# Layer norms that scale and split two feature blocks per operation, and an output projection whose last part accumulates onto a seeded PSUM bank

## The chip, the cores and the metric

The kernel runs on one core of one Trainium2 chip. A core has a matrix engine (TensorE, PE in the profile; its weight loads are the row PEld), three engines for elementwise work (VectorE is DVE, ScalarE is ACT, GpSimd is POOL) and SyncE (SP), which only issues DMAs here. Each engine works through its own queue in order and waits on semaphores for the others. Matmuls write to PSUM; everything else lies in SBUF. The metric is the device time of one execution in microseconds, lower is better.

## The reference

One inference step of a hybrid encoder layer over 576 tokens (512 of a prompt, 64 of a sample), model width 1024:

```
h   = x @ W_in                                  # heads of two kinds of attention
mix = concat(ForgettingAttention, SparseAttention)     # 1024 wide
x   = LN1(alpha * x + mix @ W_o)
x   = LN2(alpha * x + relu(x @ W_up)^2 @ W_down)       # hidden width 4096
x   = x + sigmoid(x @ W_g + b_g) * (p @ W_ple)
LN(x) = (x - mean(x)) * rsqrt(var(x) + eps) * g + b    # over the 1024 features of a token
```

All data are float32. The two layer norms, the `mix @ W_o` in front of LN1 and what surrounds them are what matters here.

## The kernel before

**Layout.** Features lie on the partitions, tokens along the free dimension: `Y` is 128 x 8 x 576, eight blocks `j` of 128 features. A token half is 288 wide (`A` is tokens 0 to 287, `B` the rest; for LN2 `A2` is 256 and `B2` 320 wide). Every matmul operand is split into a high part (rounded to the reduced format of the matmul) and a low part (the rest), and a product is three matmuls: high x high, high x low, low x high. `BH` and `BL` are the two parts of the activations; `whl` holds both parts of a weight block, made from the DMA's `wraw` by one ScalarE cast (L149) and one VectorE subtraction (L155).

**The stretch around LN1.** `wo1` multiplies six of the eight 128-row blocks of `W_o` and adds ALPHA times the residual, so that `Y` holds the residual with most of the projection. `wo2(hs, ln, steps)` does the last two row blocks for one token half: for each pair of feature blocks twelve matmuls into one PSUM tile, then VectorE adds that tile to `Y` (L1263), and the layer norm's running sum over the blocks is updated (`ln.add`). `wo2` runs for half A, then for half B, then `ple()` computes `p @ W_ple`: eight feature blocks, twelve matmuls each, and ScalarE copies each result to `PL` (L1276). Then `up(0)` starts the feed-forward: half A, then half B, and in each half the features are taken in four pairs `kp`, all four output blocks per pair.

**The layer norm** (`LayerNorm.steps`) runs beside these matmuls, one step per yield. TensorE forms the mean with a matmul by a constant (L1180), VectorE subtracts it (L1184), ScalarE squares (L1186, L1189), VectorE sums (L1190, L1159), TensorE forms the variance (L1200), ScalarE and VectorE its inverse root (L1202, L1203), TensorE spreads it over the partitions (L56, `n<-ident,ln_r`), into PSUM. Then for each pair of feature blocks: `scale` multiplies by `g` and by the inverse root, `high` adds `b` and rounds into `BH`, `low` adds `b` and subtracts `BH` into `BL`. All three take one feature block per instruction because `g` and `b` are one column each. Last, `bias` adds `b` to `Y` itself.

**PSUM tiles in turn.** `psum_g()` hands out three tiles in turn: two of one pool (`m`) and, on every third call from the second on, one of another (`psB`). Calls 1 to 4 are `wo2(A)`, 5 to 8 `wo2(B)`, 9 to 16 the eight blocks of `ple`, 17 and 18 the two tiles of `up(0)` on half A. A tile can be written again only when the instruction that empties it is done: call 11 waits for what empties call 8, and call 17 (a `psB` tile) for what empties call 14, which is block 5 of `ple`.

**What sets the order.** The code is written as generators that are interleaved (`drive`), evacuations are queued with `later`, and a scheduler then puts each engine's instructions in one fixed order. At run time every engine follows that order.

Of the kernel before, what the change touches and what calls it, by code (L numbers as in the profile page):

```python
# [10 lines left out]
AF = mybir.ActivationFunctionType  # L11
OP = mybir.AluOpType
# [19 lines left out]
HW = NT // 2  # L32
# [4 lines left out]
def tile_hybrid_step(ctx: ExitStack, tc: tile.TileContext, I, O):  # L37
    nc = tc.nc
    PE, ACT, DVE, POOL, SP = nc.tensor, nc.scalar, nc.vector, nc.gpsimd, nc.sync
# [4 lines left out]
    def f(ap):  # L44
        return ap.bitcast(F32)
# [7 lines left out]
    gb = base.tile([128, 5, 8], F32, name="gb")  # L53

    def transpose(out, in_, n):
        PE.transpose(out, in_, ident[:n, :n])  # L56
# [5 lines left out]
    def later(delay, fn):  # L62
        number[0] += 1
        evq.append((clock[0] + delay, number[0], fn))
# [216 lines left out]
    def gemm(ps, W, kmap, aH, aL, cols, yield_every=6, first=True, last=True, wc=slice(0, 128), k0=0, more=False,  # L281
             pin=False):

        n = len(kmap) * 3
        i = 0
        for kw, ka in enumerate(kmap, k0):
            for w, a in ((0, aH), (0, aL), (1, aH)):
                mm = PE.matmul(ps, W(w, kw, wc), a[:, ka, cols], start=(first and i == 0), stop=(last and i == n - 1),  # L288
                               skip_group_check=more)
                if pin:  # L290
                    tc.keep_in_program_order(mm)
                i += 1
                if i % yield_every == 0:
                    yield 1
# [561 lines left out]
    BH = BL = None  # L856
# [197 lines left out]
    for p in range(7):  # L1054
        if p == 1:
# [3 lines left out]
            BH = base.tile([128, 8, NT], F32R, name="BH", tag="BH")  # L1059
            BL = base.tile([128, 8, NT], F32R, name="BL", tag="BL")  # L1060
# [5 lines left out]
        if p == 5:  # L1066
            Y = base.tile([128, 8, NT], F32, name="Y", tag="Y")
# [55 lines left out]
    def psum_g():  # L1123
        turn[0] += 1
        if turn[0] % 3 == 2:
            return psB.tile([128, 2, 512], F32, name="g", tag="g", bufs=1)
        return psM.tile([128, 2, 512], F32, name="g", tag="m", bufs=2)

    def psum_n():
        return psN.tile([128, 512], F32, name="n", tag="n", bufs=2)  # L1130
# [3 lines left out]
    class LayerNorm:  # L1134
# [37 lines left out]
        def steps(self):  # L1172
            sl, gi, w = self.sl, self.gi, self.w
            y = Y[:, :, sl]
            while self.sums < 6:
                yield 1
            for _ in range(self.waits[0]):
                yield 1
            mu = psum_n()[:, :w]
            PE.matmul(mu, onesm, self.s[:, 0], start=True, stop=True)  # L1180
            mb = mu[:, None, :].to_broadcast([128, 2, w])
            ss = self.s
            for j in range(0, 8, 2):
                DVE.tensor_tensor(y[:, j:j + 2], y[:, j:j + 2], mb, OP.subtract)  # L1184
                if j == 0:
                    ACT.activation(ss, y[:, 0:2], AF.Square)  # L1186
                else:
                    sq = lnp[0].tile([128, 2, 320], F32, name="ln_sq", bufs=2)[:, :, :w]
                    ACT.activation(sq, y[:, j:j + 2], AF.Square)  # L1189
                    DVE.tensor_tensor(ss, ss, sq, OP.add)  # L1190
                if j == 6:
                    self.fold(ss)
                yield 1
            for _ in range(self.waits[1]):
                yield 1
            cs = [min(c, w - 128) for c in range(0, w, 128)]
            m = len(cs)
            var = psum_n()
            for i, c in enumerate(cs):
                PE.matmul(var[:, i:i + 1], ss[:, 0, c:c + 128], onesm[:, 0:1], start=True, stop=True)  # L1200
            rt = lnp[0].tile([128, 4], F32, name="ln_r", bufs=2)
            ACT.activation(rt[:, :m], var[:, :m], AF.Sqrt, bias=epst[:, 0:1])  # L1202
            DVE.reciprocal(rt[:, :m], rt[:, :m])  # L1203
            for _ in range(self.waits[2]):
                yield 1
            rb = psum_n()[:, :w]
            for i, c in enumerate(cs):
                transpose(rb[:, c:c + 128], rt[:, i:i + 1].to_broadcast([128, 128]), 128)

            def scale(j):  # L1210
                for x in (j, j + 1):
                    DVE.scalar_tensor_tensor(y[:, x], y[:, x], gb[:, gi, x:x + 1], rb, op0=OP.mult, op1=OP.mult)

            def high(j):
                for x in (j, j + 1):
                    ACT.activation(BH[:, x, sl], y[:, x], AF.Identity, bias=gb[:, gi + 1, x:x + 1])

            def low(j):
                for x in (j, j + 1):
                    DVE.scalar_tensor_tensor(BL[:, x, sl], y[:, x], gb[:, gi + 1, x:x + 1], f(BH[:, x, sl]),  # L1220
                                             op0=OP.add, op1=OP.subtract)
                self.ready += 1

            def bias(j):
                for x in (j, j + 1):
                    ACT.activation(y[:, x], y[:, x], AF.Identity, bias=gb[:, gi + 1, x:x + 1])

            scale(0)
            high(0)
            yield 1  # L1230
            scale(2)
            high(2)
            low(0)
            yield 1
            for j in (4, 6):
                scale(j)
                high(j)
                yield 1
                low(j - 2)
                yield 1  # L1240
            low(6)
            yield 1
            for _ in range(self.waits[3]):
                yield 1
            for j in range(0, 8, 2):
                bias(j)
                yield 1

    def wo2(hs, ln, steps):
        for j in range(0, 8, 2):  # L1250
            m = psum_g()
            for x in range(2):
                cs = slice((j + x) * 128, (j + x + 1) * 128)
                for k in (6, 7):
                    W = unit_w(U["ok", k], U["ok", 6])
                    for _ in gemm(m[:, x, :HW], W, (0,), BH[:, k:k + 1], BL[:, k:k + 1], hs,
                                  first=(k == 6), last=(k == 7), wc=cs):
                        pass
                WT.step(steps)
                yield 1  # L1260

            def ev(j=j, m=m):
                DVE.tensor_tensor(Y[:, j:j + 2, hs], m[:, :, :HW], Y[:, j:j + 2, hs], OP.add)  # L1263
                ln.add(j)
            later(0, ev)

# [349 lines left out]
    L1B = LayerNorm(B, 0, (3, 8, 7, 12))  # L1616
    L1 = both(L1A, L1B)
    drive(wo2(A, L1A, 3), 8, None, 0)
    early = lnp[0].tile([128, 4], F32, name="ln_r", bufs=2)
    ACT.activation(early[:, 0:1], epst, AF.Sqrt, bias=epst[:, 0:1])  # L1620
    drive(seq(wo2(B, L1B, 1), ple()), 24, L1, 24, False)
    drive(up(0, (L1A, L1B)), 16, L1, 16, False)
    XS = sums_of_x()
# [185 lines left out]
```

## Time and profile before

| | |
|---|---|
| median of three runs | 766.06 us (766.03 to 766.62) |
| the profiled execution | 765.42 us, span of its instructions 763.7 us |
| granted TensorE clock | 1.000 |
| busy: PE, DVE, ACT, POOL | 750.7, 580.3, 465.5, 111.2 us |
| first matmul of `wo2(A)`, of `ple`, of `up(0)` | 300.80, 314.01, 329.88 us |
| LN2 and the gate | about 653 us to the end |

A row of the timeline reads: start and length in us, engine, line, operation, output<-inputs, shape, count; in brackets the idle time before it and what ended it. Instructions on one engine overlap a little, so a group of two of 0.64 us takes 1.17 us: what an instruction costs in a row of its kind is the step from one start to the next. Matmuls overlap by more: each is about 0.29 us long, and one starts every 0.13 us.

### The profile page before, as it was taken

Reading aid. Unit: us, or ns where it says so; the run is one execution under the profiler, and the core shown is the slowest. Engines: PE = TensorE matmul, PEld = TensorE weight load, DVE = VectorE, ACT = ScalarE, POOL = GpSimd, SP = SyncE. Lnnn points to the kernel's source line nnn. Section 1 sums busy time; section 2 is a strip of 40 time slices with the busy share of each in tenths; the row PEclk is TensorE's granted clock in tenths of the full one; section 3 lists DMA queues with packets and bytes.
Section 4 is the critical chain, followed back from the end, with each engine's and each line's share of the span. In section 5 each row is a group of like instructions: output and inputs, shape, how many; then the busy total and the mean of one; then the engine's idle time right before and its main releaser. Section 6 shows DMA issues by size and latency. Waiting matters only on the chain.

```text
span 763.7 us, 14649 instructions
## 1 busy us (share of the span) xinstructions
PE 750.7 (98%) x5679; PEld 730.9 (96%) x5679; DVE 580.3 (76%) x1158; ACT 465.5 (61%) x933; POOL 111.2 (15%) x130
## 2 busy tenths in 40 slices
PE   9999999999999999999999999999999999999997
PEld 7999988999899999999999999999999999999997
DVE  6788888888777766998877579866898666658653
ACT  6579777887676534488654577436663466525451
POOL 7100324344241000100000000000000000010100
PEclk9999999999999999999999999999999999999999
DMA  8538354245222325243646666667666664730001
GB/s 290 169 67 151 127 144 120 90 139 172 90 82 86 106 61 176 92 170 84 139 111 174 150 160 172 147 165 179 153 153 173 152 160 152 275 125 29 30 28 69
DMA packets 38197, 101.35 MB, mean 133 GB/s; under 512 B 6000, under 2 KB 10224, under 8 KB 38000
## 3 DMA queue, kind: packets, MB, share of 16 engines
q1 hardware_dynamic: 34384, 87.61, 37.5%
q0 software_dynamic: 3456, 12.58, 10.1%
q8 instruction: 44, 0.72, 0.4%
q10 hardware_dynamic: 288, 0.22, 0.1%
q14 instruction: 25, 0.20, 0.1%
HBM read 85.26 MB, written 9.54 MB: 124 GB/s over the span
## 4 chain that ended last, share of the span: by engine, by line
PE 78%; DVE 14%; ACT 6%; issue 2%; DVEq 0%; ACTq 0%
PE g L288 41%; PE m L288 14%; PE n L288 13%; PE T L56 2%; DVE dbias L693 2%; ACT xr L771 2%; DVE whl L155 2%; DVE m L691 1%; PE V L958 1%; ACT whl L149 1%; PE m L452 1%; DVE sP L891 1%; PE m L466 1%; DVE x L774 1%; PE S L883 1%
## 5 line engine op out<-in xcount | busy, mean ns | idle before, releaser
L149 ACT CAST whl<-wraw 128x1024 fp32r<-128x1024 f32 (+2 forms) x190 | 155.0, 828 | 81.2 <-PE g L288 46.8
L155 DVE TENSOR_TENSOR whl<-wraw,whl 128x1024 fp32r<-128x1024 f32 (+2 forms) x158 | 157.7, 1008 | 48.5 <-ACT whl L149 47.9
L288 PE MATMUL m<-AH,whl 128*128 128x288 f32 x736 | 176.7, 307 | 0.0
L288 PE MATMUL g<-BH,whl 128*128 128x288 f32 (+2 forms) x768 | 160.2, 298 | 0.0
L288 PEld LDWEIGHTS m<-AH,whl 128*128 128x128 f32 x736 | 126.6, 189 | 1.7 <-issue 1.0
L288 PEld LDWEIGHTS g<-BH,whl 128*128 128x128 f32 x768 | 125.1, 189 | 1.5 <-DVE whl L155 0.2
L288 PE MATMUL g<-BL,whl 128*128 128x288 f32 (+2 forms) x384 | 113.2, 296 | 0.0
L288 PE MATMUL m<-AL,whl 128*128 128x288 f32 x368 | 108.9, 296 | 0.0
L288 PEld LDWEIGHTS g<-BL,whl 128*128 128x128 f32 x384 | 72.4, 189 | 0.2
L288 PEld LDWEIGHTS m<-AL,whl 128*128 128x128 f32 x368 | 69.7, 189 | 0.6
L210 POOL DMA_DIRECT2D wraw<-in_w_dram x24 | 20.7, 863 | 287.3 <-DMA wraw<-in_w_dram 176.3
L896 ACT ACTIVATE sP<-sP,st 128x128 f32<-128x128 f32 (+4 forms) x72 | 39.5, 550 | 35.1 <-DVE st L891 35.0
L155 POOL TENSOR_TENSOR whl<-wraw,whl 128x512 fp32r<-128x512 f32 x32 | 42.2, 1334 | 89.1 <-ACT whl L149 84.9
L288 PE MATMUL m<-BH,whl 128*128 128x288 f32 x192 | 43.0, 302 | 0.0
L288 PE MATMUL g<-s,whl 128*128 128x288 f32 x288 | 42.1, 295 | 0.0
L288 PE MATMUL n<-BH,whl 128*128 128x288 f32 x192 | 42.0, 295 | 0.0
L288 PEld LDWEIGHTS g<-s,whl 128*128 128x128 f32 x288 | 39.5, 188 | 0.0
L56 PE MATMUL T<-ident,sP 128*128 128x128 f32 (+1 forms) x176 | 31.3, 274 | 1.5 <-DVE sP L905 0.6
L288 PEld LDWEIGHTS m<-BH,whl 128*128 128x128 f32 x192 | 32.1, 188 | 0.5 <-issue 0.3
L288 PEld LDWEIGHTS n<-BH,whl 128*128 128x128 f32 x192 | 32.0, 188 | 0.0
L1481 ACT ACTIVATE g<-n 128x288 f32<-128x288 f32 x24 | 9.5, 395 | 35.6 <-PE n L288 35.6
L288 PE MATMUL m<-BL,whl 128*128 128x288 f32 x96 | 28.3, 295 | 0.0
(325 smaller groups left out, 1627.8 us busy)
## 6 DMA issues: line engine op xcount, KB each, us to landing
wraw<-in_w_dram SPq DMA_DIRECT2D x48, 512.0 KB, 3.8
wraw<-in_w_dram POOLq DMA_DIRECT2D x24, 512.0 KB, 5.7
wraw<-in_w_qkv_dram SPq DMA_DIRECT2D x23, 512.0 KB, 3.7
wraw<-in_w_dram SPq DMA_DIRECT2D x24, 256.0 KB, 4.1
wraw<-in_w_up_dram SPq DMA_DIRECT2D x8, 512.0 KB, 3.6
wraw<-in_w_down_dram SPq DMA_DIRECT2D x8, 512.0 KB, 4.3
wraw<-in_w_gate_dram SPq DMA_DIRECT2D x8, 512.0 KB, 4.4
wraw<-in_w_o_dram SPq DMA_DIRECT2D x8, 384.0 KB, 3.1
```

The costliest lines, as they stand in the source:

```text
L56: PE.transpose(out, in_, ident[:n, :n])
L149: ACT.copy(self.hv[u][:, 0, c], src["tile"][:, c])
L155: eng.tensor_tensor(t[:, 1, c], src["tile"][:, c], f(t[:, 0, c]), OP.subtract)
L210: POOL.dma_start(t[:, :n], it["acc"], accum_op=OP.add)
L288: mm = PE.matmul(ps, W(w, kw, wc), a[:, ka, cols], start=(first and i == 0), stop=(last and i == n - 1), skip_group_check=more)
L452: PE.matmul(mk[:, h, :HW], w0(part, k), a[:, k, h * HW:(h + 1) * HW], start=(k == 0 and i == 0), stop=(k == 7 and i == 2))
L466: PE.matmul(acc[b][:n[b], :304], a[:, k, b * 128:b * 128 + n[b]], ixw(part, k), start=(k == 0 and i == 0), stop=(k == 7 and i == 2))
L691: tc.keep_in_program_order(DVE.max(m, s))
L693: tc.keep_in_program_order(DVE.match_replace(out=s, in_to_replace=m, in_values=s, imm_value=GONE))
L771: q(lambda r=r, s=s: ACT.mul(v2(xr[r * 32:r * 32 + 32]), v[s * 32:s * 32 + 32], sc))
L896: ACT.activation(j["P"], j["P"], AF.Exp, bias=j["st"][:, 0:1], scale=-1.0, accum_out=j["st"][:, 2:3])
L1481: ACT.mul(P.e, P.o, -1.0)
```

## The change

In `LayerNorm.steps`, `scale` multiplies a pair of feature blocks by the inverse root alone in one VectorE instruction. `high` becomes three ScalarE instructions: two that compute `g * y + b` in place in `Y`, one per feature block with `g` as scale and `b` as bias, and one cast of the pair into `BH`. `low` is one VectorE subtraction over the pair. The separate `bias` instructions, the waits ahead of them and their steps are gone.

In `wo2`, ScalarE first copies the pair of `Y` blocks into the PSUM tile (`prepare`, one tile ahead), all twelve matmuls accumulate onto it, and ScalarE copies the sum back to `Y`. Only the second tile that is handed out is not seeded and keeps the VectorE addition.

```diff
+            rb2 = rb[:, None, :].to_broadcast([128, 2, w])
+
             def scale(j):
-                for x in (j, j + 1):
-                    DVE.scalar_tensor_tensor(y[:, x], y[:, x], gb[:, gi, x:x + 1], rb, op0=OP.mult, op1=OP.mult)
+                DVE.tensor_tensor(y[:, j:j + 2], y[:, j:j + 2], rb2, OP.mult)
 
             def high(j):
                 for x in (j, j + 1):
-                    ACT.activation(BH[:, x, sl], y[:, x], AF.Identity, bias=gb[:, gi + 1, x:x + 1])
+                    ACT.activation(y[:, x], y[:, x], AF.Identity, bias=gb[:, gi + 1, x:x + 1], scale=gb[:, gi, x:x + 1])
+                ACT.copy(BH[:, j:j + 2, sl], y[:, j:j + 2])
 
             def low(j):
-                for x in (j, j + 1):
-                    DVE.scalar_tensor_tensor(BL[:, x, sl], y[:, x], gb[:, gi + 1, x:x + 1], f(BH[:, x, sl]),
-                                             op0=OP.add, op1=OP.subtract)
+                DVE.tensor_tensor(BL[:, j:j + 2, sl], y[:, j:j + 2], f(BH[:, j:j + 2, sl]), OP.subtract)
                 self.ready += 1
-
-            def bias(j):
-                for x in (j, j + 1):
-                    ACT.activation(y[:, x], y[:, x], AF.Identity, bias=gb[:, gi + 1, x:x + 1])
...
-            for _ in range(self.waits[3]):
-                yield 1
-            for j in range(0, 8, 2):
-                bias(j)
-                yield 1
+
+    placed = [0]
 
     def wo2(hs, ln, steps):
+
+        def prepare(j):
+            m = psum_g()
+            placed[0] += 1
+            seeded = placed[0] != 2
+            if seeded:
+                ACT.copy(m[:, :, :HW], Y[:, j:j + 2, hs])
+            return m, seeded
+
+        nxt = prepare(0)
         for j in range(0, 8, 2):
-            m = psum_g()
+            m, seeded = nxt
+            if j < 6:
+                nxt = prepare(j + 2)
...
-                                  first=(k == 6), last=(k == 7), wc=cs):
+                                  first=(k == 6 and not seeded), last=(k == 7), wc=cs, more=seeded):
...
-            def ev(j=j, m=m):
-                DVE.tensor_tensor(Y[:, j:j + 2, hs], m[:, :, :HW], Y[:, j:j + 2, hs], OP.add)
+            def ev(j=j, m=m, seeded=seeded):
+                if seeded:
+                    ACT.copy(Y[:, j:j + 2, hs], m[:, :, :HW])
+                else:
+                    DVE.tensor_tensor(Y[:, j:j + 2, hs], m[:, :, :HW], Y[:, j:j + 2, hs], OP.add)
                 ln.add(j)
             later(0, ev)
```

The line numbers behind this place move by 8 in the changed kernel (the `PL` copy is L1276 before and L1284 after). Three places show how the order moves.

ScalarE while `ple` runs, from the squares of half B to the last `PL` copy. Before, the copies of blocks 5 and 6 stand behind two roundings into `BH`:

```order
L1189 ACTIVATE ln_sq<-Y 128x2x288 x2
L1276 COPY PL<-g 128x576
L149 CAST whl<-wraw 128x1024
L1189 ACTIVATE ln_sq<-Y 128x2x288
L1216 ACTIVATE BH<-Y,gb 128x288 x2
L1276 COPY PL<-g 128x576 x2
L1216 ACTIVATE BH<-Y,gb 128x288 x2
L1202 ACTIVATE ln_r<-n,epst 128x3
L1276 COPY PL<-g 128x576
```

After, on the same engine at the same place (the first `PL` row is block 4, the second block 5):

```order
L1189 ACTIVATE ln_sq<-Y 128x2x288 x2
L1284 COPY PL<-g 128x576
L1217 ACTIVATE Y<-Y,gb 128x288 x3
L1218 CAST BH<-Y 128x2x288
L1217 ACTIVATE Y<-Y,gb 128x288 x2
L1218 CAST BH<-Y 128x2x288
L1217 ACTIVATE Y<-Y,gb 128x288 x2
L1218 CAST BH<-Y 128x2x288
L1217 ACTIVATE Y<-Y,gb 128x288
L1284 COPY PL<-g 128x576
L1218 CAST BH<-Y 128x2x288
L1284 COPY PL<-g 128x576
```

Between the copies of block 4 and block 5 now stand eight scale-and-bias instructions and three casts; before, one weight cast, one square and two roundings stood there.

TensorE over the same stretch, before; `g<-pT` are the matmuls of `ple`, the rows between them are the layer norms' own matmuls (mean of B, variance of A, spread of A, variance of B):

```order
L288 MATMUL g<-pT,whl 128x288 x40
L1180 MATMUL n<-ln_s,onesm 128x288
L1200 MATMUL n<-onesm,ln_s 128x1 x3
L288 MATMUL g<-pT,whl 128x288 x16
L56 MATMUL n<-ident,ln_r 128x128 x3
L288 MATMUL g<-pT,whl 128x288 x40
L1200 MATMUL n<-onesm,ln_s 128x1 x3
```

And after:

```order
L288 MATMUL g<-pT,whl 128x288 x38
L1180 MATMUL n<-ln_s,onesm 128x288
L1200 MATMUL n<-onesm,ln_s 128x1 x3
L288 MATMUL g<-pT,whl 128x288 x19
L56 MATMUL n<-ident,ln_r 128x128 x3
L288 MATMUL g<-pT,whl 128x288 x39
L1200 MATMUL n<-onesm,ln_s 128x1 x3
```

The same matmuls, with the layer norm's moved by one or two places.

## The prediction

> **What bounds the kernel now.** I read the page first, then TensorE's waits.
>
> ```profile
> span 763.7 us, 14649 instructions
> PE 750.7 (98%) x5679; PEld 730.9 (96%) x5679; DVE 580.3 (76%) x1158; ACT 465.5 (61%) x933; POOL 111.2 (15%) x130
> ...
> PE 78%; DVE 14%; ACT 6%; issue 2%; DVEq 0%; ACTq 0%
> ```
>
> TensorE has work in flight for 98% of the span and carries 78% of the chain that ended last. Work taken off VectorE or ScalarE is worth only what it takes out of TensorE's waits. The waits of TensorE, longest first, show how little that is in the places which the change touches:
>
> ```profile
> PE V L332 <- DVE warm L304: 1.5, 1, 1.5
> PE n L288 <- DVE whl L155: 1.1, 2, 0.5
> ...
> PE g L288 <- DVE Y L1263: 0.8, 1, 0.8
> PE n L288 <- DVE hC L1325: 0.8, 2, 0.4
> ```
>
> Only the third, 0.8 us, lies at `wo2`. LN2 shows none, and the windows of that stage agree:
>
> ```profile
> 690.00:715.00 25.00, 25.00 (x184) 24.83 (x183) 19.27 (x31) 11.76 (x23) 3.97 (x2) 1.00 0.01 5
> 715.00:735.00 20.00, 20.00 (x164) 20.00 (x163) 14.69 (x29) 13.64 (x26) 0.00 (x0) 1.00 0.08 27
> ```
>
> The first number after the stretch is its length and the second PE's busy time: they are equal. So the change can only show where `ple` runs into `up(0)`. TensorE there, from the first matmul of `ple` to the last before `up(0)`, and the piece of the chain behind it:
>
> ```profile
> 314.01 3.34 PE L288 MATMUL g<-pT,whl 128*128 128x288 f32 x24
> 318.16 2.39 PE L288 MATMUL g<-pT,whl 128*128 128x288 f32 x16 [0.81 <-DVE Y L1263]
> 320.39 0.65 PE L1180 MATMUL n<-ln_s,onesm 128*128 128x288 f32 x2
> 320.88 0.73 PE L1200 MATMUL n<-onesm,ln_s 128*128 128x1 f32 x6
> 321.46 2.37 PE L288 MATMUL g<-pT,whl 128*128 128x288 f32 x16
> 323.67 0.49 PE L56 MATMUL n<-ident,ln_r 128*128 128x128 f32 x3
> 323.92 5.54 PE L288 MATMUL g<-pT,whl 128*128 128x288 f32 x40
> 329.29 0.73 PE L1200 MATMUL n<-onesm,ln_s 128*128 128x1 f32 x6
> ...
> ```
> ```profile
> 330.02 8.53 PE g L288 x61
> ```
>
> Start to start, a matmul of `ple` costs (329.29 - 323.92) / 40 = 0.134 us, the mean 0.49, a variance 0.58, the spread 0.25. `up(0)` starts at 329.29 + 0.59 = 329.88.
>
> **The change part by part.**
>
> *VectorE* loses 64 one-block operations and gets 32 two-block ones, and loses seven additions of `wo2`.
>
> ```profile
> 311.81 1.42 DVE L1184 TENSOR_TENSOR Y<-Y,n 128x576 f32<-128x576 f32 x2 [0.53 <-PE n L1180]
> 317.36 0.75 DVE L1263 TENSOR_TENSOR Y<-g,Y 128x576 f32<-128x576 f32 x1
> 329.17 0.94 DVE L1220 SCALAR_TENSOR_TENSOR BL<-Y,gb,BH 128x288 fp32r<-128x288 f32 x2
> ```
>
> Two one-block operations step 2 x 0.43 = 0.86 us, one two-block operation 0.67. That is 32 x 0.19 + 7 x 0.67 = 10.8 us less on VectorE. I put it at nothing, because the work that covers it is TensorE's; the one place where VectorE held TensorE is the next term.
>
> *The wait at 318.16.* Tile 11 of the rotation waits for VectorE's last addition of `wo2(B)`, which ended at 318.11 because it stood behind subtractions and sums of LN1. After, ScalarE copies that tile out behind three squares, at about 315, so this wait goes. Matmul 25 could have started at 314.01 + 24 x 0.134 = 317.23: 0.93 us won, if nothing later takes it.
>
> *ScalarE* gets 14 copies and 16 casts and loses 32 activations. Its rows of before, which give the steps; the idle times in brackets show how close to full it is:
>
> ```profile
> 322.81 0.64 ACT L1276 COPY PL<-g 128x576 f32<-128x576 f32 x1 [0.91 <-PE g L288]
> 323.35 0.69 ACT L1186 ACTIVATE ln_s<-Y 128x576 f32<-128x576 f32 x1
> 323.94 1.25 ACT L1189 ACTIVATE ln_sq<-Y 128x576 f32<-128x576 f32 x2
> 325.08 0.63 ACT L1276 COPY PL<-g 128x576 f32<-128x576 f32 x1
> 325.60 1.06 ACT L149 CAST whl<-wraw 128x1024 fp32r<-128x1024 f32 x1
> 326.56 0.69 ACT L1189 ACTIVATE ln_sq<-Y 128x576 f32<-128x576 f32 x1
> 327.14 0.95 ACT L1216 ACTIVATE BH<-Y,gb 128x288 fp32r<-128x288 f32 x2
> 327.99 1.17 ACT L1276 COPY PL<-g 128x576 f32<-128x576 f32 x2
> ...
> 335.11 1.81 ACT L1226 ACTIVATE Y<-Y,gb 128x288 f32<-128x288 f32 x4
> ...
> 344.85 0.66 ACT L1327 CAST hA<-hF 128x576 fp32r<-128x576 f32 x1
> 345.41 0.65 ACT L1365 ACTIVATE relu<-g 128x576 f32<-128x576 f32 x1
> ```
> ```profile
> L1481 ACT ACTIVATE g<-n 128x288 f32<-128x288 f32 x24 | 9.5, 395 | 35.6 <-PE n L288 35.6
> ```
>
> Steps: `PL` copy 0.53, square 0.58, weight cast 0.96, one-block activation with a column of bias (1.81 - 0.53) / 3 = 0.43, cast of a pair 345.41 - 344.85 = 0.56.
>
> *The seeds.* A copy of this size into PSUM isn't in the trace. Below it I put the copy of the same size out of PSUM, 0.63 us, above it twice the 288-wide PSUM-to-PSUM row, 2 x 0.395 = 0.79; I take 0.65, nearer the same size.
>
> ```profile
> 300.80 0.30 PE L288 MATMUL g<-BH,whl 128*128 128x288 f32 x1
> ```
> ```profile
> 301.25 0.75 DVE L1102 SCALAR_TENSOR_TENSOR Y<-Y,m 128x576 f32<-128x576 f32 x1
> ```
> ```profile
> 301.79 1.03 ACT L149 CAST whl<-wraw 128x1024 fp32r<-128x1024 f32 x1
> ```
>
> The tightest is the third tile: VectorE frees it at 302.0, ScalarE is through its cast at 302.8, the seed is there at 303.5, and TensorE needs it after 24 matmuls of 0.13, at 304.0. Cost 0; the cover is 0.5 us, and what runs over it would be swallowed by the wait that follows.
>
> *`high` and the queue behind it.* This term decides. `up(0)` starts on call 17 of the rotation, which needs the `PL` copy of block 5. In the new order that copy stands behind nearly the whole `high` of half A. Behind the waiting matmul stands all the rest of TensorE's queue, and for `up(0)` half A wait ScalarE's relus and all that follows.
>
> The new scale-and-bias activation has two column operands, which no row shows. What one column costs can be bounded: a 288-wide activation without one takes 0.395; the 576-wide square without one takes 0.69, and taking off 0.63 - 0.395 = 0.24 for the width leaves 0.45; with one column it takes 0.53. So a column costs 0.08 to 0.13, or nothing if the second is read beside the first. I take 0.08, from the SBUF rows, nearest in kind. The Trainium skill, "ScalarE: Activation LUTs", section "What ACT_TABLE_LOAD costs", gives about 93 ns for each column operand; by that the term below would be 0.74 in place of 0.64.
>
> Now the replay. TensorE starts `ple` at 314.01 as before, runs 38 of its matmuls (5.09), mean (0.49) and variance (0.58) and is at 320.17; block 3 is done after ten more, 321.51, plus 0.16 for the last one's length over its step, and its copy starts 0.1 later: 321.8. From there ScalarE runs without a gap: copy of block 3 0.53, four squares 2.32 with a weight cast 0.96 among them, copy of block 4 0.53, eight activations 3.44 and three casts 1.68, then the copy of block 5 0.64. Sum 10.10 + 8 x 0.08 for the second column = 10.74; it ends at 332.54.
>
> TensorE meanwhile finishes the other 9 of the 19, spread, 39 matmuls and variance: 320.17 + 2.55 + 0.25 + 5.23 + 0.59 = 328.79. It waits 3.8 us and starts `up(0)` at 332.6, where it started at 329.88 before: 2.7 us later. The 0.93 us won above is swallowed by this wait.
>
> *Given back.* The 61 matmuls after 329.88 took 8.50 us (to 338.38) where 61 x 0.134 is 8.17: TensorE ran close behind LN1 there. After, `BL` is nearly done when `up(0)` starts, so 0.3 comes back. Half B of LN1 has the same longer `high`, but its spread stands 42 matmuls into `up(0)` (338.2) and half B of `up(0)` follows after 96 (345.5); its eight activations and four casts, 8 x 0.51 + 4 x 0.56 = 6.3 us, fit between. Cost 0.
>
> *LN2* gets the same edits: its pairs come sooner from VectorE and later from ScalarE. With no TensorE wait in the two windows and ScalarE busy 25.4 of 45 us I take 0, with 0.3 above for the last half.
>
> *Bias steps gone:* 32 activations of 0.43 leave ScalarE, behind the point that decides, and what they made way for (the sums of `x` for the next stage) only comes earlier. No DMA is added or moved past another. Cost 0.
>
> Sum: +2.7 - 0.3 = +2.4 us. The profiled execution of 765.42 (1.7 more than its span) becomes 767.8; it lies 0.64 under the median, so the median becomes 766.06 + 2.4 = 768.5, 0.3% slower. A difference of 0.2% (1.5 us) is about what can be told here from no change.
>
> **The rivals.**
>
> *Faster: the block-5 copy isn't late.* If ScalarE's chain of 10.74 us ran in under 6.9, `up(0)` would start at 328.8, 1.1 us early; with the 0.3 that is 766.06 - 1.4 = 764.7. The turning point is a chain of 8.3 us. For it: the copies could be as quick as the 0.395 of L1481. Against: every step is from a row of its own size.
>
> *No change: given back later.* The waits for `hC` and `whl` add up to 1.9 us after `up(0)`. If weights and not TensorE set them, a later start meets shorter waits: 768.5 - 1.9 = 766.6. Against: `hC` is made from matmul results just before, so it moves with TensorE.
>
> *Slower still: the clock.* The warm-up matmuls at the start, 512 wide, step 4.02 / 9 = 0.447 us, where 0.134 per 288 would be 0.238:
>
> ```profile
> 1.53 4.02 PE V L332 x9
> ```
>
> So TensorE starts at about half pace. If a pause of 3.8 us sends it back there for as long, nine times 0.21 is 1.9 us more: 770.4. Against: no pause of the trace is as long, and the clock reads 1.00 throughout. The Trainium skill, "TensorE: Matmul & The Clock Gate", section "Why this matters for your kernels", warns of this for pauses over about 3 us; its section "What's actually happening" asks for a whole idle window of 3.4 us on a free-running count, which a pause this long would seldom cover. No trace here shows either.
>
> **How the numbers follow.** The likeliest case, the late copy, has 0.66: its own range is 767.5 (second column free, casts 0.1 shorter) to 769.2 (0.13 per column, LN2 at its upper end). The copy in time has 0.10, given back later 0.14, the clock 0.10. A range of 766.4 to 770.0 leaves out the copy in time, part of the clock's case, and some spill. The copy in time, 1.4 us faster, lies at the bound of 1.5: half of it counts as faster, half as the same. With 0.04 of the likeliest and the case given back that makes 0.23 for the same, 0.05 for faster, 0.72 for slower.
>
> **What would show it.** TensorE: the bracket `DVE Y L1263` at 318 gone, and one wait of 3 to 4 us before 332.6 ended by ScalarE's `PL` copy (now L1284); `up(0)` from there without small waits; all later stages shifted by 2.4 us and otherwise alike. ScalarE: no idle time from 321.8 to 332.5, L1217 near 0.61, L1218 near 0.66, seeds (L1249) near 0.65. Wrong if TensorE's longest wait there is under 2 us, if its waits for `hC` and `whl` shrink, or if matmuls after the wait step about 0.26 for some microseconds.

## The result and the profile after

| | before | after |
|---|---|---|
| median | 766.15 us (766.03 to 766.62, 6 runs) | 770.25 us (770.04 to 771.23, 6 runs) |
| ratio | | 1.0056, interval 1.0043 to 1.0069 |
| profiled execution, span | 765.42, 763.7 us | 770.04, 768.3 us |
| granted clock, mean | 1.000 | 0.997 |

The change makes the kernel 4.1 us slower. 2.4 us were forecast, from one late copy; the copy is late as forecast, and TensorE's clock halves behind it, which the forecast gave one chance in ten.

From the page of after, the busy times:

```profile
PE 752.3 (98%) x5679; PEld 731.9 (95%) x5679; DVE 572.6 (75%) x1119; ACT 472.3 (61%) x931; POOL 109.2 (14%) x130
```

VectorE is busy 7.7 us less than before, ScalarE 6.8 us more, and the span is longer. The waits of TensorE, of after:

```profile
PE g L288 <- ACT PL L1284: 3.5, 1, 3.5
PE V L332 <- DVE warm L304: 1.5, 1, 1.5
PE n L288 <- DVE whl L155: 1.1, 2, 0.5
...
PE n L288 <- DVE hC L1333: 0.8, 2, 0.4
```

The wait for `Y` (0.8 us) is gone; one for the copy of `PL` stands on top; `whl` and `hC` are as they were. TensorE's timeline over the same stretch as in the prediction:

```profile
314.62 5.21 PE L288 MATMUL g<-pT,whl 128*128 128x288 f32 x38
319.82 0.75 PE L1180 MATMUL n<-ln_s,onesm 128*128 128x288 f32 x2
320.41 0.72 PE L1200 MATMUL n<-onesm,ln_s 128*128 128x1 f32 x6
321.00 2.76 PE L288 MATMUL g<-pT,whl 128*128 128x288 f32 x19
323.59 0.49 PE L56 MATMUL n<-ident,ln_r 128*128 128x128 f32 x3
323.84 5.42 PE L288 MATMUL g<-pT,whl 128*128 128x288 f32 x39
329.13 0.83 PE L1200 MATMUL n<-onesm,ln_s 128*128 128x1 f32 x6
333.47 0.61 PE L288 MATMUL g<-BH,whl 128*128 128x288 f32 x1 [3.51 <-ACT PL L1284]
333.88 0.44 PE L288 MATMUL g<-BL,whl 128*128 128x288 f32 x1
334.12 0.68 PE L288 MATMUL g<-BH,whl 128*128 128x288 f32 x2
334.60 0.44 PE L288 MATMUL g<-BL,whl 128*128 128x288 f32 x1
```

`ple` starts 0.61 us later than in the trace of before; the first matmul of `wo2(A)` is as much later (301.41), and a kernel below without any part of the change (the pause of 4.65 us) starts both at the same two times, so this isn't the change's. The profiled execution of before was itself 0.64 us under the median of its three runs. `up(0)` starts at 333.47, 3.59 later than before, so 2.98 of it belongs to this stretch. Behind the pause the matmuls step 0.24 us in place of 0.134 (333.88 to 334.12). The windows of this trace around it; the column behind POOL's is the granted clock:

```profile
329.65:333.06 3.41, 0.31 (x3) 0.23 (x3) 3.23 (x5) 3.41 (x8) 0.00 (x0) 1.00 0.00 0
333.06:336.48 3.42, 3.01 (x12) 3.01 (x13) 1.45 (x4) 3.10 (x6) 0.00 (x0) 0.50 0.79 209
```

TensorE works 0.31 of the first 3.41 us. In the second 3.42 us the clock is 0.50, and 12 matmuls run in 3.0 us. 12 x (0.24 - 0.134) = 1.3 us is what this costs. The trace records the change of clock at 333.06 and back at 336.48 exactly, and no other between 5.4 us, where it turns full, and the last two microseconds. So in this trace: 2.98 late, 1.3 at half clock, a few tenths given back.

Two of the six runs read 771.23 and 0.995, the others 770.04 to 770.30 and 0.997. A second stretch at half clock would fit the two; they have no trace.

ScalarE, of after, from the copy of block 3 to the copy of block 5:

```profile
322.60 0.64 ACT L1284 COPY PL<-g 128x576 f32<-128x576 f32 x1 [1.17 <-PE g L288]
...
326.40 0.62 ACT L1284 COPY PL<-g 128x576 f32<-128x576 f32 x1
326.92 1.67 ACT L1217 ACTIVATE Y<-Y,gb 128x288 f32<-128x288 f32 x3
328.49 0.66 ACT L1218 CAST BH<-Y 128x576 fp32r<-128x576 f32 x1
...
332.27 0.63 ACT L1217 ACTIVATE Y<-Y,gb 128x288 f32<-128x288 f32 x1
332.80 0.62 ACT L1284 COPY PL<-g 128x576 f32<-128x576 f32 x1
```

From 322.60 to 333.42 it runs without a gap: 10.82 us, where 10.74 was forecast.

### The profile page after: what moved, and what is told of

It reads as the page before. It is cut to its first block, busy times and chain, and to the rows that moved or that the text cites. A ratio compares the mean times of both kernels' runs of the same rounds, so it can differ in the third digit from the quotient of the medians.

```text
span 768.3 us, 14628 instructions
## 1 busy us (share of the span) xinstructions
PE 752.3 (98%) x5679; PEld 731.9 (95%) x5679; DVE 572.6 (75%) x1119; ACT 472.3 (61%) x931; POOL 109.2 (14%) x130
## 4 chain that ended last, share of the span: by engine, by line
PE 78%; DVE 12%; ACT 7%; issue 2%; DMA 1%; ACTq 0%; DVEq 0%
PE g L288 41%; PE m L288 14%; PE n L288 13%; DVE dbias L693 2%; PE T L56 2%; ACT xr L771 2%; DVE m L691 1%; DVE whl L155 1%; PE V L958 1%; ACT whl L149 1%; PE m L452 1%; PE m L466 1%; DVE sP L891 1%; DVE x L774 1%; PE S L883 1%
## 5 line engine op out<-in xcount | busy, mean ns | idle before, releaser
L155 DVE TENSOR_TENSOR whl<-wraw,whl 128x1024 fp32r<-128x1024 f32 (+2 forms) x158 | 159.5, 1019 | 55.4 <-ACT whl L149 54.7
```

Of the source, the lines that this page charges most:

```text
L155: eng.tensor_tensor(t[:, 1, c], src["tile"][:, c], f(t[:, 0, c]), OP.subtract)
```

## The experiments

The theory after the trace: the copy of block 5 is late because of its place in ScalarE's order (about 2.5 us), and the pause that this makes lowers TensorE's clock (about 1.5 us). The first rival (C in the expectations): the clock has another cause, or is an accident of these executions, and the late start alone makes the loss. The second (A): the longer `high` as such, or LN2, costs the time. The third (B): ScalarE's two copies per tile in `wo2` do. The kernels ran in three sets, each with runs of the kernel before beside it; their median is given behind "against", and the ratios go by it.

### One part alone

The layer norms changed and `wo2` as before, then the reverse (the two hunks of the diff, one left out each time).

> Only the layer norms are changed; wo2 is as before. In ScalarE's order the copy of ple block 5 stands behind six scale-and-bias activations and two casts (eight and three in the full change). Theory (late copy, and a half clock after a pause of about 3.4 us): TensorE keeps the 0.8 us wait for VectorE's addition at 318, then waits about 2 us for the copy; the pause is too short for the clock to fall; 766.15 + 1.7 = 767.9, clock 1.00. Rival A (the layer norm's longer high is to blame as such, wherever the copy stands): as slow as the full change, 770. Rival B (the two ScalarE copies per tile in wo2 are to blame): 766.

Measured: 768.83 us (767.69 to 769.17) against 765.72, ratio 1.0038 (1.0025 to 1.0051). The loss is 3.1 us where 1.7 was expected (the set's runs of before lie lower than the 766.15 of the expectation), because the clock falls here too. By its time alone this kernel lies between the theory and rival A, and it is the kernels below that tell the two apart. TensorE's timeline of this kernel, and the two windows around its start of `up(0)`:

```profile
329.64 0.72 PE L1200 MATMUL n<-onesm,ln_s 128*128 128x1 f32 x6
332.42 0.40 PE L288 MATMUL g<-BH,whl 128*128 128x288 f32 x1 [2.06 <-ACT PL L1267]
...
333.64 0.45 PE L288 MATMUL g<-BL,whl 128*128 128x288 f32 x1
333.88 0.69 PE L288 MATMUL g<-BH,whl 128*128 128x288 f32 x2
```
```profile
329.79:333.20 3.41, 1.35 (x13) 1.27 (x12) 3.40 (x5) 3.41 (x7) 0.00 (x0) 1.00 0.18 30
333.20:336.61 3.41, 3.41 (x17) 3.41 (x16) 2.52 (x4) 3.41 (x7) 0.00 (x0) 0.50 1.02 314
```

A pause of 2.06 us was enough, in a window in which TensorE works 1.35 of 3.41 us. Four of the five runs have 0.997 and 768.63 to 769.17 us; the fifth has 0.999 and 767.69, about 1.2 less.

> Only wo2 is changed (seeds and copies back by ScalarE); the layer norms are as before. The copies of ple blocks 5 and 6 stand right behind one rounding. Theory: the wait for VectorE's addition at 318 goes and nothing takes its place: 766.15 - 1.2 = 765.0, clock 1.00, no TensorE wait over 0.3 us between 314 and 345. Rival B (ScalarE's copies are to blame): slower than before, 768 or more. Rival A: as the theory.

Measured: 764.59 us (764.28 to 765.08) against 765.72, ratio 0.9986 (0.9977 to 0.9995): faster than both. The wait for `Y` is gone and nothing takes its place. From the start of `ple` to the start of `up(0)` it takes 329.52 - 314.34 = 15.18 us, before 15.87. TensorE's timeline of this kernel at the two places:

```profile
314.34 5.21 PE L288 MATMUL g<-pT,whl 128*128 128x288 f32 x38
...
329.52 0.51 PE L288 MATMUL g<-BH,whl 128*128 128x288 f32 x2
```

The two parts are not additive: -1.1 and +3.1 make +2.0, not +4.1. With the seeds TensorE is at the pause earlier, and in the order of the whole change block 5's copy stands behind eight activations and three casts, in that of the layer norms alone behind six and two.

### The copy of block 5 placed first

The whole change, and `PL` copies of blocks 5 to 7 get a higher rank in the scheduler.

```diff
-            later(0, lambda j=j, m=m: ACT.copy(PL[:, j]..., m[:, :, :HW]))
+            def out(j=j, m=m):
+                with tc.high_priority() if j >= 5 else ExitStack():
+                    ACT.copy(PL[:, j]..., m[:, :, :HW])
+            later(0, out)
```

> The full change, with the copies of ple blocks 5, 6 and 7 put ahead in ScalarE's order, each as soon as its matmuls are done: block 5 behind two activations, block 6 behind three more and a cast. Nothing else is moved by hand. Theory (late copy): no pause of 3 us, a wait of about 1 us in ple instead, clock 1.00, 766.15 - 0.2 = 766.0 (765.4 to 766.6). Rival A (the longer high as such): up(0) waits for BH and BL instead, 768 or more. Rival C (half clock without a pause): 767.5.

Measured: 765.96 us (765.44 to 766.20) against 765.72, ratio 1.0003 (0.9994 to 1.0012), clock 1.0. ScalarE's timeline of this kernel, then TensorE's:

```profile
326.27 0.62 ACT L1286 COPY PL<-g 128x576 f32<-128x576 f32 x1
326.79 1.15 ACT L1217 ACTIVATE Y<-Y,gb 128x288 f32<-128x288 f32 x2
327.83 0.62 ACT L1286 COPY PL<-g 128x576 f32<-128x576 f32 x1
```
```profile
328.51 1.86 PE L288 MATMUL g<-pT,whl 128*128 128x288 f32 x12 [0.97 <-ACT PL L1286]
330.21 0.72 PE L1200 MATMUL n<-onesm,ln_s 128*128 128x1 f32 x6
330.79 0.38 PE L288 MATMUL g<-BH,whl 128*128 128x288 f32 x1
```

Every operation of the change is there and the loss of 4.1 us is not. What made it is the place of these copies, of block 5's above all, for which `up(0)` waited. Against the new projection alone (764.59) the new layer norms still cost 1.4 us in this order, most of it in the 0.97 us wait.

### The second column left out

The whole change, with `g` left out of `high`, so that the layer norms don't multiply by it.

```diff
-   ACT.activation(y[:, x], y[:, x], AF.Identity, bias=gb[:, gi + 1, x:x + 1], scale=gb[:, gi, x:x + 1])
+   ACT.activation(y[:, x], y[:, x], AF.Identity, bias=gb[:, gi + 1, x:x + 1])
```

> The whole change, but the activation of high has no second column (the scale g is left out of the layer norms, so the output isn't the reference's). In the order that comes out, ScalarE copies block 5 after two activations of high, not after eight. My theory: the lateness comes from the place of that copy, which a small change of one operand moves; up(0) starts within 0.5 us of before, no pause over 1.2 us, clock full, 765.6 (765.0 to 766.2). Rival: the time of high itself on ScalarE makes up(0) late wherever the copy stands: 768 or more. L1217 should fall from 0.63 to about 0.53 us, which gives the second column's price.

Measured: 765.41 us (765.07 to 765.78) against 765.95, ratio 0.9994 (0.9985 to 1.0003), as expected. The group of `high`'s activations in after and in this kernel (mean ns behind the busy time), then ScalarE's timeline of this kernel:

```profile
L1217 ACT ACTIVATE Y<-Y,gb 128x288 f32<-128x288 f32 x16 | 9.2, 621 | 5.6 <-DVE Y L1213 5.6
```
```profile
L1217 ACT ACTIVATE Y<-Y,gb 128x288 f32<-128x288 f32 x16 | 7.7, 531 | 2.0 <-DVE Y L1213 2.0
```
```profile
325.97 0.63 ACT L1284 COPY PL<-g 128x576 f32<-128x576 f32 x1
326.49 0.96 ACT L1217 ACTIVATE Y<-Y,gb 128x288 f32<-128x288 f32 x2
327.36 0.63 ACT L1284 COPY PL<-g 128x576 f32<-128x576 f32 x1
```

The column costs 621 - 531 = 90 ns, 0.7 us on the eight. But without it the fixed order comes out otherwise: the copy of block 5 stands behind two activations and ends at 327.99, not at 333.42. The eight columns are 0.7 us at most of these 5.4; the rest is order. `up(0)` starts earlier than expected, 14.46 us behind the start of `ple` where before took 15.87, in part because TensorE's order has moved too: one matmul of `up(0)` now stands ahead of the variance of half B, and the next follows at 15.23.

### The pause filled

The whole change, with 20, 16 or 10 matmuls behind the variance of half B whose result nobody reads. ScalarE and the start of `up(0)` are not touched; only TensorE's idle time is shorter.

```diff
+            if gi == 0 and sl.start:
+                for _ in range(20):
+                    PE.matmul(var[:, 128:128 + HW], PT2[:, 0, 0, 0:128], PT2[:, 0, 0, 0:HW], start=True, stop=True)
```

> The full change, and 20 matmuls of ple's operands into unused columns of a PSUM tile (their result is not used) behind the variance of half B, where TensorE would pause. They take 20 x 0.134 = 2.7 us of the 3.75 us pause, and up(0) still starts when the copy of block 5 is done. Theory (the pause lowers the clock): one wait of about 1.1 us is left, clock 1.00, 770.25 - 1.3 = 768.9. Rival C (the half clock has another cause, not the pause): clock 0.997 as before, 770.2 or more.

Measured: 768.23 us (768.12 to 768.72) against 765.72, ratio 1.0033 (1.0021 to 1.0046), clock 1.0:

```profile
329.43 2.88 PE L1203 MATMUL n<-pT 128*128 128x288 f32 x20
333.08 0.40 PE L288 MATMUL g<-BH,whl 128*128 128x288 f32 x1 [0.77 <-ACT PL L1287]
```

TensorE does 20 matmuls more, and the loss is 2.5 us in place of 4.1. That is the price of the late copy alone, with the clock kept. This is the strongest evidence that the other 1.6 us are the clock. The last full window of this trace, in which the program ends, shows besides that the clock stays when 47% of a window is idle (TensorE works 1.80 of 3.41 us): in the row that follows, the granted clock still reads 1.00.

```profile
760.40:763.81 3.41, 1.80 (x13) 1.54 (x11) 1.03 (x4) 0.68 (x2) 0.00 (x0) 1.00 0.14 48
763.81:766.50 2.69, 0.00 (x0) 0.00 (x0) 0.00 (x0) 0.00 (x0) 0.00 (x0) 1.00 0.20 61
```

> The whole change, with 10 matmuls whose result nobody reads (288 wide, into columns of the variance's tile that nobody uses) behind the variance of LN1 half B, so that TensorE's pause ahead of up(0) is 2.2 to 2.4 us in place of 3.5; up(0) starts when it did. If the clock falls when a window of 3.4 us is mostly idle, wherever the window falls on the program: most executions at 0.997 and 769.2 to 769.7, some at 1.0 and 768.2, as with the two-block layer norm alone, where a pause of 2.06 us lowered it in four of five. If it needs a pause of 3 us or a wholly idle window: 768.2 in all, clock 1.0.

Measured: 769.91 us (769.61 to 771.02) against 765.95, ratio 1.0056 (1.0044 to 1.0069); all five runs at 0.996 or 0.997. The pause is 2.08 us, a little shorter than planned. The theory expected a run or two at 1.0; there was none. The window ahead of the half clock in this kernel:

```profile
329.55:332.96 3.41, 1.32 (x11) 1.09 (x9) 3.02 (x4) 3.41 (x8) 0.00 (x0) 1.00 0.00 0
```

> The same with 16 such matmuls: pause 1.4 to 1.6 us. If the clock falls only when well over half of a 3.4 us window is idle: 768.2 and clock 1.0 in all executions. If it falls for pauses of this length too: some executions at 769.4 and 0.997.

Measured: 768.65 us (767.87 to 768.96) against 765.95, ratio 1.0033 (1.0021 to 1.0046). Its trace has the full clock, with a pause of 1.30 us, also shorter than planned. Two of the runs (768.65 and 768.96) read 0.998, too near the others to tell.

### A pause alone, in the kernel before

No part of the change: GpSimd makes ten, or six, additions, and a one-column matmul that nobody reads waits for them a few matmuls into `up(0)`.

```diff
                 if j == 6:
                     self.fold(ss)
+                    if gi == 0 and sl.start:
+                        hold = lnp[0].tile([128, 320], F32, name="hold", bufs=1)[:, :w]
+                        POOL.tensor_tensor(hold, ss[:, 0], ss[:, 0], OP.add)
+                        for _ in range(9):
+                            POOL.tensor_tensor(hold, ss[:, 0], hold, OP.add)
...
+            if gi == 0 and sl.start:
+                PE.matmul(var[:, 4:5], hold[:, 0:128], onesm[:, 0:1], start=True, stop=True)
```

The kernel with six additions comes first; "the same" in its expectation is the kernel with ten, which stands behind it.

> The same with six additions: pause 1.5 to 2.1 us at about 333. If the clock falls only when well over half of a window is idle: mostly before + the pause, 767.6 to 768.1, clock 1.0, with an execution or another at 0.997 and about 1.2 more, as the two-block layer norm alone had at 2.06. If pauses of this length lower it always: 768.8 to 769.3 in all.

Measured: 770.27 us (768.61 to 770.55) against 765.82, ratio 1.0051 (1.0038 to 1.0063). The pause came out at 2.54 us, longer than planned. Two runs have 1.0 and 768.61 and 768.83, three have 0.996 to 0.998 and 770.27 to 770.55. One program, the same pause, and 1.4 to 1.9 us between the two kinds of run. The traced one kept its clock:

```profile
334.85 0.38 PE L1207 MATMUL n<-onesm,hold 128*128 128x1 f32 x2 [2.54 <-POOL hold L1197]
```
```profile
330.41:333.82 3.41, 1.88 (x12) 1.42 (x11) 3.41 (x5) 2.39 (x5) 3.17 (x4) 1.00 0.72 283
333.82:337.23 3.41, 2.38 (x18) 2.38 (x19) 3.41 (x6) 1.96 (x6) 0.90 (x2) 1.00 0.18 28
```

Here the boundary of two windows fell into the pause, and neither window is more than half idle.

> The kernel before with a pause alone: GpSimd makes ten additions behind the last sum of squares of LN1 half B, and a one-column matmul that nobody reads waits for them, some 12 matmuls into up(0). Layer norms and projection are as before, so ScalarE and VectorE are not later. Pause 3.3 to 4 us at about 336. If the pause alone costs its length: before + 3.3 to 4.0 with clock 1.0, 769.2 to 769.9. If the clock halves for what is left of a window of 3.4 us behind it: 1.0 to 1.6 more, clock 0.997, 770.5 to 771.5, matmuls behind the wait stepping 0.24 us.

Measured: 774.35 us (774.13 to 775.35, 4 runs) against 765.82, ratio 1.0110 (1.0094 to 1.0125); 8.5 us more. The pause is 4.65 us in the trace, which is of the slowest of the four runs (775.35). Pause and time of the expectation are too low, and its clock is too high: in the trace it is halved for three windows, not one.

```profile
339.55 0.58 PE L1207 MATMUL n<-onesm,hold 128*128 128x1 f32 x2 [4.65 <-POOL hold L1197]
```
```profile
332.50:335.91 3.41, 1.67 (x9) 0.96 (x7) 3.41 (x3) 0.86 (x3) 3.17 (x4) 1.00 0.29 112
335.91:339.32 3.41, 0.00 (x0) 0.00 (x0) 2.94 (x5) 0.00 (x0) 3.17 (x4) 0.50 0.47 154
339.32:342.74 3.42, 3.19 (x13) 3.19 (x14) 0.58 (x2) 2.57 (x7) 0.17 (x1) 0.50 0.00 0
342.74:346.15 3.41, 3.41 (x17) 3.41 (x16) 2.70 (x4) 1.52 (x4) 0.00 (x0) 0.50 0.21 55
```

The first window is half idle, the second wholly, and the third and fourth are still slow while TensorE is busy. Why the fourth is slow, when after's clock was back one window behind its pause, stays open.

The two kernels make a little more than a pause, and of the expectation's "ScalarE and VectorE are not later" the part on VectorE doesn't hold: beside GpSimd's additions two of VectorE's subtractions for `BL` take 2.05 and 2.07 us, where two took 0.94 before. With six additions TensorE doesn't wait for them. With ten it does, for 0.73 us ahead of the pause, and these waits are part of the first window's idle half. VectorE's timeline of the kernel with ten, then TensorE's:

```profile
332.23 2.07 DVE L1227 SCALAR_TENSOR_TENSOR BL<-Y,gb,BH 128x288 fp32r<-128x288 f32 x2
```
```profile
333.38 0.40 PE L288 MATMUL g<-BL,whl 128*128 128x288 f32 x1 [0.42 <-DVE BL L1227]
334.36 0.40 PE L288 MATMUL g<-BL,whl 128*128 128x288 f32 x1 [0.31 <-DVE BL L1227]
```

That idle time of TensorE costs its length and then a stretch at half clock is shown all the same, in kernels without any part of the change.

### LN2 by itself

The new projection, LN1 as before, LN2 changed: `scale`, `high`, `low` and `bias` of before stand under `if gi == 0`, the new ones under `else`.

> LN1 as in the kernel before (both halves), LN2 with the new two-block operations, and the new output projection. My theory: LN2's change costs nothing, and all the loss of the change is made in LN1 half A; so this runs as the kernel with the new projection alone, 764.6 (764.0 to 765.2), no wait of TensorE at up(0), clock full. Rival: LN2's longer work on ScalarE costs what it saves on VectorE and more (my bound was 0.3): 764.9 or later. Second rival: the VectorE time saved in LN2 helps: under 764.2.

Measured: 764.90 us (764.28 to 765.47) against 765.95, ratio 0.9987 (0.9978 to 0.9995); the projection alone had 0.9986. (764.90 is also where the rival's times began, but this set's runs of before lie 0.23 higher.) LN2's part is worth nothing either way, and the whole loss is made in LN1.

## Why the prediction was wrong in size

- *The place and the copy: right.* One wait, ended by ScalarE's `PL` copy of block 5, longest of all of TensorE's; shown to be the copy's place by the kernel that moves it first. The chain was 10.82 us for 10.74 forecast, `up(0)` 2.98 us late for 2.7. Kept at full clock the loss is 2.5 us, for +2.4 forecast.
- *The second column: right within 0.01.* 90 ns, 0.08 taken. The Trainium skill, "ScalarE: Activation LUTs", section "What ACT_TABLE_LOAD costs", gives about 93 ns for each column; the rows agree. What the prediction didn't see is that this column also moved the copy.
- *The clock: the step that failed.* The sum has no term for it. It was a rival at 0.10, whose 770.4 lay outside the range, on the argument that the clock needs "a whole idle window of 3.4 us on a free-running count, which a pause this long would seldom cover". The count is free-running: in twelve traces the clock turns full between 4.2 and 6.9 us after the start of the program, and all stretches at one clock that begin and end inside the program last 1, 3, 96, 97, 125, 126 or 221 to 223 times 3.413 us. But the window need not be wholly idle. It was 91, 60 and 61% idle where the clock fell in after, in the layer norms alone and with ten fillers, and about half (51%) with the pause of 4.65 us; it stayed with 47% and less. A pause of 3.51 us, wherever the windows lie, puts at least half of itself, 1.76 us or 51%, into one of them, which fits that all six runs fell. The sign that the prediction named for this case, matmuls that step about 0.26 us behind the wait, came with 0.24. The Trainium skill, "TensorE: Matmul & The Clock Gate", section "What's actually happening", states the window of 3413 ns, its free run and two clocks a factor of two apart, and the traces agree with all three (3.413 us, 4.2 to 6.9, 0.50 and 1.00); its "≥1 idle window" is what they contradict, if idle means without work.
- *The price of the clock: over-sized.* 1.9 us was taken from the warm-up matmuls. One window at half clock can't cost more than half of 3.41, 1.7; measured were 1.3 in the trace and 1.6 between the kernels. With it the forecast's terms make 766.06 + 2.4 + 1.6 = 770.1.
- *"Against: no pause of the trace is as long, and the clock reads 1.00 throughout."* True from 5.9 us on, where the trace of before records the clock as full (the slow warm-up matmuls lie ahead of it), and no evidence: a trace without a pause says nothing of what a pause does.
- *Seeds, VectorE's wait, LN2, given back later: right.* Seeds (L1249) 0.64 us for 0.65 and no wait of TensorE at `wo2`; the wait for `Y` gone and swallowed, and worth 1.1 us where no pause follows (the projection alone); LN2 0; `hC` and `whl` unchanged, so nothing was given back there.
- *VectorE's saving* was 7.7 us of busy time; the 10.8 of the forecast were counted in steps. It hid behind TensorE as said, so the size didn't matter.

## What to carry to other kernels

When an instruction gets one operand more, or an engine gets work from another, look in the order for what now stands behind it: here one 0.63 us copy that fell behind eight activations and three casts made the whole loss, and the new projection by itself, 0.14% faster than before, is the version to keep. Price a new pause of TensorE as its length and, from about 2 us on, about half of a clock window more (the pause of 4.65 us cost more than that); matmuls that nobody reads are a cheap test of which of the two one sees.

## What the hardware showed

- The clock fell after pauses of 2.06, 2.08, 3.51 and 4.65 us (and in three of five runs at 2.54), not in the traces with 0.77, 0.97 and 1.30; what decides by these traces is how much of one 3.41 us window is idle (51% and more lowered it, 47% and less did not), and so the same program can do either.
- After a pause of 4.65 us the clock was half for three windows, two of them with TensorE busy for 93% and all of the time.
- A ScalarE activation that is 288 wide takes 531 ns with one column operand and 621 with two.
- Beside GpSimd's additions two 288-wide subtractions of VectorE took 2.05 and 2.07 us, without them 0.94.
